# Interleaving the rounded and rest weights of a projection word by word in one SBUF tile

## The chip, the cores and the metric

The kernel runs on one core of a Trainium2 chip. The time is that of the device, in microseconds (us), from one launch; the median of several runs is quoted. A profiled execution of the same program gives the trace: start and length of each instruction on each engine. TensorE (PE in the rows) multiplies, and its weight loads have a track of their own (PEld). ScalarE is ACT, VectorE is DVE, GpSimd is POOL, and SyncE is SP, which here issues DMA transfers.

## The reference

One step of a decoder layer for 256 prompt tokens and 8 sample tokens (264 together) with a model width of 2048. An RMS-normed input goes through a wide input projection. Two branches follow, sparse attention (compressed, selected and window keys, with a cache of 2048 past tokens for each sample) and a gated delta rule. Each branch is gated and projected back, the two are merged by sigmoid gates, and an output projection is added to the residual:

```python
(q_a, kvc, kvs, kvw, g_nsa, z_a, qkv_b, a_b, b_b, z_b, gate_a, gate_b) = split_proj(rms_norm(x_p, norm_w) @ w_in)
...
y_a = nsa_merge(o_cmp, o_slc, o_win, g_nsa, z_a, w_pa)
y_b, S_p, conv_p = gdn_branch(qkv_b, a_b, b_b, z_b, zero_conv, zero_S, *gw)
m = jax.nn.sigmoid(gate_a) * y_a + jax.nn.sigmoid(gate_b) * y_b
return x + m @ w_o
```

The compressed keys and values come from a learned map over the cache: rows of 16 tokens times `w1` (first product), a SiLU, and `w2` (second product).

## The kernel before

All arithmetic is done in float32 quality. A matmul on type `fp32r` keeps fewer bits, so each operand is cut in two: a rounded part (`hi`, a copy on ScalarE to type fp32r) and the rest (`lo`, the original minus `hi`, on VectorE). A product is then three matmuls that add up in PSUM, hi by hi, hi by lo and lo by hi (`three`).

The projections are a list of *half units*, `halves`. A half unit `W` is a block of 1024 rows by 128 columns of a weight matrix (72 columns for the small projection `wsm`), stored as 128 partitions by 8 chunks by 128. Its `load` issues one DMA of 512 KB to the tile `raw`. Its `split` allocates `hi` and `lo` and fills them: one ScalarE copy of 1024 elements per partition (L324) and one VectorE subtraction (L325). Its `mms` runs 24 matmuls, 8 chunks by three products: the weights are `hi[:, k, :]` or `lo[:, k, :]`, the streamed operand is a 264-column slice of `xh`/`xl` (input projection), `oh`/`ol` (branch outputs) or `mh`/`ml` (merged output). In the rows "acc<-xl,hi" is a matmul that streams `xl` past the weights `hi`; weights stand last. All matmuls are issued by the helper at L197, transposes by L194.

`CQ` units do the first product of the compression. There `hi` and `lo` hold the cache rows, 256 or 288 columns for each of 2 to 4 steps, and are streamed; the weights are `w1h` and `w1l`, which were split once. `W` and `CQ` take their `hi` and `lo` from the same tags, with three buffers each. The second product is in `g_cmp_fin`: for values, the weights are `hg[:, g, :]`, where

```python
hg = hs[:, :n].rearrange("p (c g) -> p g c", g=2)
...
mm(p2[0:nn, 128 * g:128 * g + 128], hg[:, g, :], P("w2v"))
```

so these weights (tile `chs`) are every second word of a row. A product of plain float32 operands is two loads and two matmuls in the trace.

The main loop at the end of `program` goes through `halves`: at step i it issues the load of half i + 4, the split of half i + 2, and the matmuls of half i in two parts, and after each part the generators of all other work (attention, delta rule, norms) may advance by one step (`tick`). SP's and GpSimd's queues are written out in program order; the order of instructions on TensorE, ScalarE and VectorE is laid out when the kernel is built.

Of the kernel before, what the change touches and what calls it, by code (L numbers as in the profile page):

```python
# [11 lines left out]
F32R = mybir.dt.float32r  # L12
# [124 lines left out]
def program(tc, A):  # L137
# [4 lines left out]
    def pool(name, bufs=1, space=None):  # L142
        p = tc.tile_pool(name=name, bufs=bufs, space=space) if space is not None else tc.tile_pool(name=name, bufs=bufs)
        ctxs.append(p)
        return p.__enter__()
# [3 lines left out]
    st = pool("st")  # L149
# [163 lines left out]
    class W:  # L313
# [5 lines left out]
            SP.dma_start(self.raw, self.src)  # L319

        def split(self):
            self.hi = st.tile([128, 8, self.cols], F32R, name="hi", tag="hi", bufs=3)
            self.lo = st.tile([128, 8, self.cols], F32R, name="lo", tag="lo", bufs=3)
            S.activation(self.hi, self.raw, AF.Copy)  # L324
            V.tensor_sub(self.lo, self.raw, self.hi)  # L325

# [56 lines left out]
    class CQ:  # L383
# [8 lines left out]
        def split(self):  # L392
            kv, b, s0, s1 = self.kv, self.b, self.s0, self.s1
            n = 256 + 32 * self.prompt
            self.hi = st.tile([128, s1 - s0, n], F32R, name="hi", tag="hi", bufs=3)
            self.lo = st.tile([128, s1 - s0, n], F32R, name="lo", tag="lo", bufs=3)
            for ph in range(2):
                src = rawc[kv, b][ph][:, :, s0:s1].rearrange("p n s c g -> p s n (c g)")
                h = self.hi[:, :, 128 * ph:128 * ph + 128].rearrange("p s (n c) -> p s n c", n=8)
                l = self.lo[:, :, 128 * ph:128 * ph + 128].rearrange("p s (n c) -> p s n c", n=8)  # L400
                S.activation(h, src, AF.Copy)  # L401
                V.tensor_sub(l, src, h)  # L402
            if self.prompt:
                h = self.hi[:, :, 256:].rearrange("p s (c g) -> p s g c", g=2)
                l = self.lo[:, :, 256:].rearrange("p s (c g) -> p s g c", g=2)
                for g in range(2):
                    src = L["kvc"][:, 2 * kv + g, 0:TP].rearrange("p (c s) -> p s c", s=16)[:, s0:s1]
                    S.activation(h[:, :, g], src, AF.Copy)
                    V.tensor_sub(l[:, :, g], src, h[:, :, g])
# [1055 lines left out]
    hl = {}  # L1465
# [145 lines left out]
    n = len(halves)  # L1611
# [117 lines left out]
```

## Time and profile before

| | |
|---|---|
| median of 3 runs | 1151.09 us (1150.13 to 1151.12) |
| profiled execution | 1147.96 us, span of its instructions 1146.2 us |
| matmuls | 9088, TensorE busy 1116.5 us (97%) |
| weight loads | 9088, busy 1090.7 us (95%) |
| VectorE, ScalarE, GpSimd | 777.0, 603.5 and 146.6 us (68%, 53%, 13%) |
| mean granted clock of TensorE | 0.996 of full speed |

Busy time is the union of an engine's instructions. Matmuls overlap in the pipeline, each is recorded longer than the distance to the next, and their ends are modelled: what a matmul costs in a stream is the distance from start to start. The recorded length of a load is longer than its distance to the next load, too.

### The profile page before, as it was taken

To read this page: it belongs to the slowest core of one execution; us is meant where nothing else is said; L and a number is where in the kernel's file an instruction comes from. 1 tells how busy PE (TensorE), PEld (TensorE's weight loads), DVE (VectorE), ACT (ScalarE), POOL (GpSimd) and SP (SyncE) were. 2 spreads that over 40 slices of the span, in tenths; PEclk is the share of its full clock that TensorE was granted. 3 is DMA by queue.
4 is the path that set the end of the run, shared out by engine and by line. 5 is a ranking of instruction groups with operands and counts; after the bars stand their busy time and mean duration, and the time that the engine had idled before them with its cause. 6 is when DMAs were issued, how large, how long until landed. Compare 5 with 4: busy or idle time off the path is not lost.

```text
span 1146.2 us, 24552 instructions
## 1 busy us (share of the span) xinstructions
PE 1116.5 (97%) x9088; PEld 1090.7 (95%) x9088; DVE 777.0 (68%) x1619; ACT 603.5 (53%) x1165; POOL 146.6 (13%) x218
## 2 busy tenths in 40 slices
PE   4999999999999999999899999999999999999998
PEld 4989999999999998998899999999999999999998
DVE  3587665444667886996888977699746685567543
ACT  4455655445635776785566644444344844454332
POOL 4430344200001311114110300100100000000000
PEclk9999999999999999999999999999999999999999
DMA  8874676335536775467996944655752555555673
GB/s 299 256 233 142 195 216 205 124 111 165 169 121 197 210 203 154 127 190 191 261 356 240 330 152 163 180 181 175 214 179 108 212 186 183 185 179 204 213 238 128
DMA packets 76842, 222.74 MB, mean 194 GB/s; under 512 B 10465, under 2 KB 27370, under 8 KB 75186
## 3 DMA queue, kind: packets, MB, share of 16 engines
q1 hardware_dynamic: 59922, 168.55, 45.5%
q0 software_dynamic: 14784, 45.61, 14.0%
q10 hardware_dynamic: 2016, 7.01, 1.6%
q8 instruction: 71, 1.16, 0.4%
q14 instruction: 49, 0.40, 0.1%
HBM read 203.14 MB, written 17.99 MB: 193 GB/s over the span
## 4 chain that ended last, share of the span: by engine, by line
PE 85%; DVE 4%; DMA 3%; issue 1%; ACT 1%; POOL 0%; ACTq 0%; POOLq 0%; DVEq 0%
PE acc L197 70%; DMA gv<-cslv,idx 2%; DVE lo L325 1%; PE po L197 1%; PE gsc L197 1%; PE gtr L194 1%; DVE lanes L1227 1%; PE ps L197 1%; PE sw L197 1%; DMA raw<-win 1%; PE inv L197 1%; PE cf L197 1%; DVE prod L1226 1%; PE pvo L197 1%; PE uw L197 1%
## 5 line engine op out<-in xcount | busy, mean ns | idle before, releaser
L324 ACT ACTIVATE hi<-raw 128x1024 fp32r<-128x1024 f32 (+1 forms) x250 | 264.1, 1056 | 328.4 <-PE acc L197 265.4
L197 PE MATMUL acc<-xh,hi 128*128 128x264 f32 (+1 forms) x1488 | 428.9, 288 | 0.3 <-ACT gate L1491 0.3
L197 PE MATMUL acc<-xl,hi 128*128 128x264 f32 (+1 forms) x1488 | 426.8, 287 | 0.0
L197 PE MATMUL acc<-xh,lo 128*128 128x264 f32 (+1 forms) x1488 | 425.6, 286 | 0.0
L325 DVE TENSOR_TENSOR lo<-raw,hi 128x1024 fp32r<-128x1024 f32 (+1 forms) x250 | 304.3, 1218 | 171.5 <-ACT hi L324 168.7
L197 PEld LDWEIGHTS acc<-xl,hi 128*128 128x128 f32 (+1 forms) x1488 | 280.6, 189 | 2.0 <-issue 0.6
L197 PEld LDWEIGHTS acc<-xh,hi 128*128 128x128 f32 (+1 forms) x1488 | 280.5, 189 | 2.0 <-ACT gate L1491 0.6
L197 PEld LDWEIGHTS acc<-xh,lo 128*128 128x128 f32 (+1 forms) x1488 | 279.6, 188 | 1.7 <-issue 0.5
L197 PE MATMUL acc<-hi,w1h 128*128 128x254 f32 (+1 forms) x512 | 147.7, 289 | 15.9 <-ACT hi L401 15.9
L197 PE MATMUL acc<-lo,w1h 128*128 128x254 f32 (+1 forms) x512 | 146.5, 286 | 3.3 <-DVE lo L402 3.1
L197 PE MATMUL acc<-hi,w1l 128*128 128x254 f32 (+1 forms) x512 | 145.1, 283 | 0.0
L402 DVE TENSOR_TENSOR lo<-rawc,hi 128x512 fp32r<-128x512 f32 (+2 forms) x136 | 84.1, 656 | 52.1 <-ACT hi L401 45.9
L197 PEld LDWEIGHTS acc<-hi,w1h 128*128 128x128 f32 x512 | 97.9, 191 | 16.0 <-ACT hi L401 15.9
L401 ACT ACTIVATE hi<-rawc 128x512 fp32r<-128x512 f32 (+2 forms) x136 | 74.7, 599 | 61.3 <-PE acc L197 56.5
L197 PEld LDWEIGHTS acc<-lo,w1h 128*128 128x128 f32 x512 | 98.6, 192 | 4.5 <-DVE lo L402 4.3
L197 PEld LDWEIGHTS acc<-hi,w1l 128*128 128x128 f32 x512 | 98.3, 192 | 0.1
L378 POOL DMA_DIRECT2D rawc<-ccmp x125 | 67.4, 539 | 97.7 <-issue 72.6
L197 PE MATMUL acc<-oh,hi 128*128 128x264 f32 x256 | 73.6, 287 | 0.2 <-ACT gate L1491 0.2
L197 PE MATMUL acc<-ol,hi 128*128 128x264 f32 x256 | 73.5, 287 | 0.0
L197 PE MATMUL acc<-oh,lo 128*128 128x264 f32 x256 | 73.4, 287 | 0.0
L197 PE MATMUL acc<-mh,hi 128*128 128x264 f32 x256 | 72.7, 284 | 0.0
L197 PE MATMUL acc<-ml,hi 128*128 128x264 f32 x256 | 72.6, 283 | 0.0
(453 smaller groups left out, 1651.9 us busy)
## 6 DMA issues: line engine op xcount, KB each, us to landing
raw<-win SPq DMA_DIRECT2D x184, 512.0 KB, 3.7
raw<-wpab SPq DMA_DIRECT2D x32, 512.0 KB, 3.3
raw<-wo SPq DMA_DIRECT2D x32, 512.0 KB, 3.5
rawc<-ccmp SPq DMA_DIRECT2D x126, 128.0 KB, 3.1
rawc<-ccmp POOLq DMA_DIRECT2D x125, 128.0 KB, 3.3
raw<-w SPq DMA_DIRECT2D x8, 512.0 KB, 5.4
wk<-winK SPq DMA_DIRECT2D x8, 512.0 KB, 9.3
o_wk<-wk POOLq DMA_DIRECT2D x8, 512.0 KB, 8.0
```

What stands on the lines that cost most here:

```text
L194: T.transpose(out, in_, ident[0:n, 0:n])
L197: T.matmul(out, lhsT, rhs, start=start, stop=stop, **k)
L324: S.activation(self.hi, self.raw, AF.Copy)
L325: V.tensor_sub(self.lo, self.raw, self.hi)
L378: e.dma_start(rawc[kv, b][j // 8][:, j % 8].rearrange("p s c g -> p (s c g)"), src[kv, bass.ds(r, 1)].rearrange("o d f -> (o d) f"))
L401: S.activation(h, src, AF.Copy)
L402: V.tensor_sub(l, src, h)
L1226: V.tensor_tensor(pp, Lt[:, 0:i, 0:i], La[:, i, 0:i, None].to_broadcast([64, i, i]), ALU.mult)
L1227: V.tensor_reduce(Lt[:, i, 0:i], pp.rearrange("p j c -> p c j"), AX.X, ALU.add, negate=True)
```

## The change

One tile per half unit takes the place of two. For `W` it is 128 partitions by 8 chunks by 128 columns by 2 words, and `hi` and `lo` are the words 0 and 1 of each pair: 8 bytes lie between one element of `hi` and the next. The copy writes with this stride, the subtraction reads `hi` and writes `lo` with it, and the weight loads read with it. The small projection uses 72 of the 128 columns. For `CQ` the tile holds first all of `hi` and then all of `lo`, each contiguous as before. The tile's tag has three buffers, as each of the two tags had. The bytes in SBUF are the same for 128-column halves.

```diff
         def split(self):
-            self.hi = st.tile([128, 8, self.cols], F32R, name="hi", tag="hi", bufs=3)
-            self.lo = st.tile([128, 8, self.cols], F32R, name="lo", tag="lo", bufs=3)
+            hl = st.tile([128, 8, 128, 2], F32R, name="hilo", tag="hilo", bufs=3)
+            self.hi, self.lo = hl[:, :, 0:self.cols, 0], hl[:, :, 0:self.cols, 1]
             S.activation(self.hi, self.raw, AF.Copy)
             V.tensor_sub(self.lo, self.raw, self.hi)
...
             n = 256 + 32 * self.prompt
-            self.hi = st.tile([128, s1 - s0, n], F32R, name="hi", tag="hi", bufs=3)
-            self.lo = st.tile([128, s1 - s0, n], F32R, name="lo", tag="lo", bufs=3)
+            hl = st.tile([128, 2, s1 - s0, n], F32R, name="hilo", tag="hilo", bufs=3)
+            self.hi, self.lo = hl[:, 0], hl[:, 1]
```

## Rows read from the trace of the kernel before

**Rows 1.** Page, busy time, share of the span, instructions of each engine.

```profile
PE 1116.5 (97%) x9088; PEld 1090.7 (95%) x9088; DVE 777.0 (68%) x1619; ACT 603.5 (53%) x1165; POOL 146.6 (13%) x218
```

**Rows 2.** Page, groups of instructions: count | busy us, mean ns | idle before, releaser.

```profile
L324 ACT ACTIVATE hi<-raw 128x1024 fp32r<-128x1024 f32 (+1 forms) x250 | 264.1, 1056 | 328.4 <-PE acc L197 265.4
...
L325 DVE TENSOR_TENSOR lo<-raw,hi 128x1024 fp32r<-128x1024 f32 (+1 forms) x250 | 304.3, 1218 | 171.5 <-ACT hi L324 168.7
```

**Rows 3.** Chain that ended last, pieces in time: start us, length us, what.

```profile
189.97 11.22 PE acc L197 x96
...
637.14 9.61 DMA raw<-win
...
932.50 210.53 PE acc L197 x1742
```

**Rows 4.** Timeline, 163.5 to 164.6 us: start us, length us, engine, instruction.

```profile
163.55 0.19 PEld L197 LDWEIGHTS acc<-hi,w1l 128*128 128x128 f32 x1
163.66 0.28 PE L197 MATMUL acc<-hi,w1l 128*128 128x254 f32 x1
163.66 0.55 PEld L197 LDWEIGHTS cf<-prm,chs 128*127 128x127 f32 x4
...
163.78 0.63 PE L197 MATMUL cf<-prm,chs 128*127 128x128 f32 x4
```

**Rows 5.** Groups by line, shapes kept apart: weight loads of half units.

```profile
L197 PEld LDWEIGHTS acc<-xl,hi 128*128 128x128 f32 x1472 | 278.3, 189 | 2.0 <-issue 0.6
...
L197 PEld LDWEIGHTS acc<-xl,hi 128*72 128x72 f32 x16 | 2.3, 142 | 0.0
```

**Rows 6.** Timeline of PE, first and last of 31 matmuls, small projection.

```profile
290.76 0.29 PE L197 MATMUL acc<-xh,hi 128*72 128x264 f32 x1
...
294.43 0.29 PE L197 MATMUL acc<-xh,hi 128*72 128x264 f32 x1
```

**Rows 7.** Timeline near 157 us: four loads in a row, few streamed columns.

```profile
157.17 0.53 PEld L197 LDWEIGHTS cf<-csq,cst 128*128 128x128 f32 x4
```

**Rows 8.** Waits: who waited for whom, us in total, times, longest.

```profile
ACT hi L324 <- PE acc L197: 265.4, 163, 6.7
...
PEld acc L197 <- DVE lo L325: 0.2, 1, 0.2
```

**Rows 9.** Instructions of the tile cf: duration ns min/median/max, start first and last.

```profile
L197 PEld LDWEIGHTS cf<-prm,chs x36: 92/196/199, 163.7 to 248.2; 128*127 128x127 f32 x32, 128*15 128x15 f32 x4
...
L197 PEld LDWEIGHTS cf<-cst,csq x32: 187/191/192, 47.7 to 157.9; 128*127 128x127 f32 x32
```

**Rows 10.** Timeline of PE, first and last of 745 matmuls.

```profile
1039.65 0.28 PE L197 MATMUL acc<-ol,hi 128*128 128x264 f32 x1
...
1129.55 0.28 PE L197 MATMUL acc<-ml,hi 128*128 128x264 f32 x1
```

**Rows 11.** Timeline, a half unit's matmul behind two transposes.

```profile
282.58 0.37 PE L197 MATMUL acc<-xl,hi 128*128 128x264 f32 x1
```

**Rows 12.** Groups by line, shapes kept apart: short copies and a subtraction.

```profile
L408 ACT ACTIVATE hi<-kvc 128x48 fp32r<-128x48 f32 x16 | 3.6, 272 | 0.0
...
L1454 ACT ACTIVATE dso<-dod 128x64 f32<-128x64 f32 x1 | 0.3, 254 | 0.0
...
L409 DVE TENSOR_TENSOR lo<-kvc,hi 128x48 fp32r<-128x48 f32 x16 | 3.0, 228 | 0.0
```

**Rows 13.** Lines L1409 and L1412: duration ns min/median/max, start.

```profile
L1409 DVE TENSOR_TENSOR wq<-wq,deb x1: 216/216/216, 664.3 to 664.3; 128x64 f32<-128x64 f32 x1
...
L1412 DVE TENSOR_TENSOR dkq<-dcv x1: 220/220/220, 664.0 to 664.0; 128x64 f32<-128x64 f32 x1
```

**Rows 14.** Timeline, one split of the last stage and its first `lo` matmul.

```profile
1050.18 1.06 ACT L324 ACTIVATE hi<-raw 128x1024 fp32r<-128x1024 f32 x1 [1.47 <-PE acc L197]
...
1051.27 1.23 DVE L325 TENSOR_TENSOR lo<-raw,hi 128x1024 fp32r<-128x1024 f32 x1
...
1056.09 0.28 PE L197 MATMUL acc<-mh,lo 128*128 128x264 f32 x1
```

## The prediction

> **What bounds the kernel now.** I read the page's busy shares first: the matmuls cover 1116.5 of 1146.2 us [rows 1]. The time is a count of matmuls times their spacing, plus some 30 us in which TensorE has nothing to run. For the count I take the groups by line: 250 copies and 250 subtractions make the weights of 250 half units [rows 2], and a half unit has 24 matmuls (`mms`, 8 chunks by three products), together 6000. The chain that ended last gives their spacing: 1742 of them in 210.53 us, 120.9 ns each, with 264 streamed columns; 96 matmuls of the compression take 11.22 us, 116.9 ns each, with 254 [rows 3]. Per streamed column that is 0.458 and 0.460 ns.
>
> A weight load runs beside each matmul. The timeline shows how they interlock: a load starts with the matmul before it or up to 0.01 us later, and the load's own matmul follows 0.11 to 0.12 us after [rows 4]. For this change all hangs on which of the two sets the 121 ns. The small projection tells: its weights have 72 columns, its loads last 142 ns where those of 128 columns last 189 [rows 5], yet 31 of its matmuls start from 290.76 to 294.43 [rows 6], 30 spacings of 122.3 ns. A load 47 ns shorter buys nothing. The matmul sets the spacing and the load has room.
>
> How much room? Loads set the pace where few columns are streamed. Four loads of 128 contiguous columns beside 15 streamed ones cover 0.53 us, the last of them 0.19: (0.53 - 0.19) / 3 = 113 ns from load to load [rows 7]. Against 121 that leaves 8 ns.
>
> The waits show who else could hold TensorE: a load waited 0.2 us, once, for a `lo` of L325, while ScalarE waited 265.4 us, 163 times, until TensorE gave a buffer back [rows 8]. The splits run ahead of their use.
>
> **The change, part by part.** *Loads.* The 6000 loads of the half units are now read with a stride of 8 bytes. The kernel before has loads of just this form: `hg[:, g, :]`, weights of the compression's second product, is every second word of `chs`. With 127 columns they last 196 ns in the median, against 191 for 127 contiguous columns of `csq` [rows 9], and four of them cover 0.55 us [rows 4]: (0.55 - 0.196) / 3 = 118 ns from load to load, against 113. So the stride costs 5 to 6 ns a load; with one column more I take a floor of 118.5 ns. That is 2.5 ns under the mean spacing. The first load of such a group runs beside a 254-column matmul, and the next matmul starts 0.12 us on (163.66 to 163.78 [rows 4]); over the six such places the starts lie 117, 118, 119, 119, 120 and, once, 209 ns apart. That is what a floor near 118.5 gives, beside a matmul at full pace.
>
> The spacings scatter, and those under the floor are lifted to it. The 745 matmuls from 1039.65 to 1129.55, first and last in [rows 10], have a mean spacing of 120.8 ns; 41 spacings are 117 ns or less, 115 are 118 or less. Raising each one under 118.5 to 118.5 adds 0.2 ns to the mean; a floor of 120 would add 0.5 and one of 121 would add 1.0. I take 0.2 ns x 6000 = 1.2 us, with 0 (the stride costs nothing) and 1.0 x 6000 = 6.0 us (the room is used up) as bounds.
>
> Where a half unit resumes behind another kind of matmul, no long matmul hides the load: the one at 282.58, behind two transposes, is recorded 0.37 us long instead of 0.28, since it waits for its weights [rows 11]. The trace has 189 such resumptions; 55 of them follow a matmul of 256 columns or more, which hides the load. The other 134 pay 6 ns each: 0.8 us, from 0 to 1.1 (all 189).
>
> The Trainium skill (SBUF — State Buffer, section "Door 1: The DMA port swizzle") gives SBUF lines of 16 bytes and says that two accesses to a line suffice to absorb its latency. An 8-byte stride leaves just two words per line, so by that page the strided loads are free and the time stays at 1151.1. The 196 against 191 ns of [rows 9] disagree, and the row decides.
>
> *ScalarE.* The copy to `hi` (1056 ns, [rows 2]) now writes with the stride. No row has that alone. The nearest is L408: 48 elements, written 8 bytes apart and read 64 bytes apart, 272 ns; 64 contiguous elements take 254 [rows 12]. Less 16 x 1.03 (1056 / 1024) that is 237 for 48, so L408 pays 35 ns, 0.73 per element. The bounds are 0 and 0.73 x 1024 = 0.74 us a copy.
>
> *VectorE.* The subtraction (1218 ns, [rows 2]) reads `hi` and writes `lo` with the stride. L1409 reads and writes 64 elements 8 bytes apart in 216 ns, and L1412 takes 220 on contiguous ones [rows 13]: nothing. L409 is 48 elements, with another operand read 64 bytes apart: 228 ns [rows 12], against 220 - 16 x 1.19 = 201, so 27 / 48 x 1024 = 0.58 us a subtraction as the upper bound. L1409 has the new form and L409 has a wider stride besides, so I take 0, and by likeness 0 for ScalarE.
>
> Both lie beside matmuls in any case. In the last stage the copy starts at 1050.18, the subtraction lasts from 1051.27 to 1052.50, and that half's first `lo` is used at 1056.09 [rows 14]: 3.6 us of cover, which is also the median when I pair all 250 halves so. At both upper bounds, 1.3 us, all but 9 stay covered. If the cover were gone, TensorE would wait for the copy and the subtraction in turn, 2.3 us.
>
> *The shared tile.* `hi` and `lo` are now given back together, at the latest when the last product has read `lo`, one spacing (0.12 us) after the last use of `hi`. The next split starts that much later, against 3.6 us of cover: 0. If a first product now had to wait for `lo` as well as for `hi`, the same cover holds: 0. In the compression units each part stays contiguous within its tile, and their weights (`w1h`, `w1l`) are not touched: 0. No DMA, no byte and no queue changes.
>
> Sum: 1.2 + 0.8 + 0 = 2.0 us on the profiled execution (1147.96 us, span 1146.2). The median of the runs lies 3.1 above that; I carry the difference over: 1151.1 + 2.0 = **1153.1 us**, 0.17% more. About 0.2%, 2.3 us, is what a measurement of this kernel can tell from no change, so the forecast is no change.
>
> **The rivals.**
> *Slower: the load becomes the pace.* A load begins with its predecessor's matmul or up to 10 ns later [rows 4]; if such a delay comes on top of the 118, the floor is 121 or more, and from there each nanosecond counts 6000 times. A floor of 121.5 adds about 1.3 ns in the mean, 7.8 + 0.8 us: 1160. If the whole 6 ns go onto each spacing it is 36 + 0.8: 1188. For it: there are 2.5 ns of room, measured on few loads. Against it: the 72-column weights and the six 254-column spacings. It decides from 121 ns on. The Trainium skill (TensorE: Matmul & The Clock Gate, section "Back-to-back issue gap") says that in a stream matmul and weight load together set the spacing; by that rule this rival is the case. The 122.3 ns of [rows 6] disagree while the load is the shorter of the two.
>
> *Slower: ScalarE and VectorE.* At the upper bounds, 0.74 + 0.58 us more per half, the nine halves with less cover than that are late by 6.6 us together: 1151.1 + 2.0 + 6.6 = 1160. L1409 speaks against it, L408 for it.
>
> *Faster: another order.* Only the queues of SP and GpSimd are written out by hand; the order on the other engines is laid out at build from the tiles and when they are given back. If one tile per half moves instructions there, a wait in the chain, such as the 9.61 us for `raw` at 637 [rows 3], may shorten; losing 5 us of it gives 1151.1 + 2.0 - 5 = 1148. It could as well grow, and nothing in the trace says that the order moves.
>
> **How the numbers follow.** Hidden loads, as summed: 0.65, with a range of its own from 1150 to 1158; 0.50 of it within 0.2%, 0.15 above. The load as the pace: 0.16. ScalarE and VectorE: 0.09. Another order: 0.10. So faster 0.10, same 0.50, slower 0.15 + 0.16 + 0.09 = 0.40. The range from 1149 to 1163 takes in the bounds of the sum and the near ends of the slower rivals; outside it I leave 0.07 of the faster case and 0.11 of the far ends of the others.
>
> **What would show it.** Right: loads of half units of about 194 instead of 189 ns, spacings of 121.0 to 121.3 ns in the long last piece of the chain, L324 and L325 still at 1056 and 1218. Wrong: a spacing of 122 ns or more there (the load sets the pace); L324 or L325 longer by 0.3 us or more, with new waits of TensorE for them; or stages in another order.

## The result

The kernel got slower: 1162.56 us in the median of four runs (1162.28 to 1164.07), against 1151.11 for the kernel before in four runs beside them. The ratio is 1.0103, with a 95% interval from 1.0086 to 1.0121: 11.45 us, 1.0%. The forecast was 1153.1 us and no change; the range from 1149 to 1163 holds the time.

The profiled execution took 1162.28 us, with a span of 1160.6. First the page's busy shares of the changed kernel, which answer to [rows 1], and its groups of instructions for the two halves of the split, which answer to [rows 2] (count | busy us, mean ns | idle before, releaser):

```profile
PE 1129.5 (97%) x9088; PEld 1103.0 (95%) x9088; DVE 779.8 (67%) x1619; ACT 625.6 (54%) x1165; POOL 146.9 (13%) x218
...
L325 DVE TENSOR_TENSOR hilo<-raw,hilo 128x1024 fp32r<-128x1024 f32 (+1 forms) x250 | 305.2, 1221 | 177.8 <-ACT hilo L324 176.1
L324 ACT ACTIVATE hilo<-raw 128x1024 fp32r<-128x1024 f32 (+1 forms) x250 | 287.3, 1149 | 215.6 <-PE acc L197 171.4
```

TensorE's busy time grew by 13.0 us with the same 9088 matmuls. Its idle time, span less busy, went from 29.7 to 31.1 us. So the loss sits inside the matmul stream, and not in new waits. The waits of TensorE confirm it (total us, times, longest):

```profile
PE acc L197 <- ACT hilo L401: 15.1, 2, 14.1
PE acc L197 <- DVE hilo L402: 4.2, 2, 3.1
PE acc L197 <- DVE gate L1498: 3.8, 3, 2.6
```

None is for L324 or L325; the 14.1 us is the wait for the first cache rows, which the kernel before has too (15.9 us). ScalarE's copy is 93 ns longer than before (1149 against 1056), VectorE's subtraction 3 ns.

Where the matmul stream lost, the chain that ended last shows (start us, length us), as in [rows 3]:

```profile
191.70 11.22 PE acc L197 x96
...
936.60 220.82 PE acc L197 x1798
```

The 96 matmuls of the compression, whose weights are contiguous in both kernels, take 11.22 us as before. The half units in the long last piece take 220.82 / 1798 = 122.8 ns each instead of 120.9. In the windows view, 90 us of that piece have no other work, and TensorE is covered throughout at full clock (columns: window, length, PE, PEld, DVE, ACT, POOL busy, PEclk, DMA share, GB/s):

```profile
1040.00:1130.00 90.00, 90.00 (x736) 90.00 (x735) 52.77 (x69) 38.07 (x40) 0.00 (x0) 1.00 0.63 217
```

The window counts 736 matmuls with those that run over its edges; 733 of them start in it, 122.8 ns apart. Before, 745 started in 89.9 us, 120.8 ns apart [rows 10]. The weight loads of the changed kernel, with shapes kept apart, answer to [rows 5]:

```profile
L197 PEld LDWEIGHTS acc<-xl,hilo 128*128 128x128 f32 x1472 | 287.5, 195 | 1.0 <-issue 0.2
L197 PEld LDWEIGHTS acc<-xl,hilo 128*72 128x72 f32 x16 | 2.3, 144 | 0.0
```

195 instead of 189 ns for 128 columns, and 144 instead of 142 for 72.

From here on a *mean spacing* is worked out from all start times of the trace: the mean from one matmul of a half unit to the next of its kind, with 128 columns of weights, leaving out the pauses (spacings over 1.3 times the median). It is 121.02 ns before and 122.86 after. 1.84 x 6000 = 11.0 us, against 11.45 measured.

### The profile page after: what moved, and what is told of

It is laid out like the page before. It is cut to its first block, busy times and chain, and to the rows that moved or that the text cites. A ratio compares the mean times of both kernels' runs of the same rounds, so it can differ in the third digit from the quotient of the medians.

```text
span 1160.6 us, 24512 instructions
## 1 busy us (share of the span) xinstructions
PE 1129.5 (97%) x9088; PEld 1103.0 (95%) x9088; DVE 779.8 (67%) x1619; ACT 625.6 (54%) x1165; POOL 146.9 (13%) x218
## 4 chain that ended last, share of the span: by engine, by line
PE 83%; DVE 5%; DMA 3%; issue 1%; ACT 1%; POOL 0%; DVEq 0%; ACTq 0%; POOLq 0%
PE acc L197 68%; DMA gv<-cslv,idx 2%; DVE hilo L325 1%; PE po L197 1%; PE gsc L197 1%; PE sw L197 1%; PE gtr L194 1%; DVE lanes L1227 1%; PE ps L197 1%; DMA raw<-win 1%; PE inv L197 1%; PE pvo L197 1%; PE cf L197 1%; PE uw L197 1%; PE wsc L197 1%
## 5 line engine op out<-in xcount | busy, mean ns | idle before, releaser
L197 PE MATMUL acc<-xh,hilo 128*128 128x264 f32 x2976 | 582.7, 290 | 0.9 <-ACT gate L1491 0.9
L197 PEld LDWEIGHTS acc<-xh,hilo 128*128 128x128 f32 x2976 | 483.0, 195 | 4.1 <-ACT gate L1491 1.2
L197 PE MATMUL acc<-xl,hilo 128*128 128x264 f32 (+1 forms) x1488 | 429.2, 289 | 0.0
L325 DVE TENSOR_TENSOR hilo<-raw,hilo 128x1024 fp32r<-128x1024 f32 (+1 forms) x250 | 305.2, 1221 | 177.8 <-ACT hilo L324 176.1
L324 ACT ACTIVATE hilo<-raw 128x1024 fp32r<-128x1024 f32 (+1 forms) x250 | 287.3, 1149 | 215.6 <-PE acc L197 171.4
L197 PEld LDWEIGHTS acc<-xl,hilo 128*128 128x128 f32 (+1 forms) x1488 | 289.8, 195 | 1.0 <-issue 0.2
L197 PE MATMUL acc<-hilo,w1h 128*128 128x254 f32 (+1 forms) x1024 | 191.8, 288 | 19.7 <-ACT hilo L401 15.1
L197 PEld LDWEIGHTS acc<-hilo,w1h 128*128 128x128 f32 x1024 | 161.5, 192 | 21.5 <-ACT hilo L401 15.3
L197 PE MATMUL acc<-hilo,w1l 128*128 128x254 f32 (+1 forms) x512 | 145.2, 284 | 0.0
L197 PEld LDWEIGHTS acc<-hilo,w1l 128*128 128x128 f32 x512 | 98.4, 192 | 0.1
```

The costliest lines, as they stand in the source:

```text
L197: T.matmul(out, lhsT, rhs, start=start, stop=stop, **k)
```

## The experiments

The expectations call the theories by letters. **A**: a strided load needs about 118 ns from load to load, and the matmul's 121 ns are too near to that; the loss is a matter of the margin between the two. **B**: each strided load costs the stream a fixed 1.8 ns, whatever stands beside it. **C**: the strided writes of ScalarE and VectorE disturb the stream. **D**: the shared tile, with its joint release and another order of instructions, costs the time. D was open, since the order did change: the matmuls of the two kernels first differ at the 694th of 9088. All ratios are against the kernel before on the same chip in the same hour (1148.40 us for the first four experiments, 1148.31 for the next four, 1148.79 for the last four).

### One shared tile, everything contiguous

```diff
-            self.hi = st.tile([128, 8, self.cols], F32R, name="hi", tag="hi", bufs=3)
-            self.lo = st.tile([128, 8, self.cols], F32R, name="lo", tag="lo", bufs=3)
+            hl = st.tile([128, 2, 8, self.cols], F32R, name="hilo", tag="hilo", bufs=3)
+            self.hi, self.lo = hl[:, 0], hl[:, 1]
```

`CQ` is edited as in the change, and the matmuls run in the order of the changed kernel.

> One tile for hi and lo, but all of hi first and then all of lo, so nothing is strided. Theories: (A) the strided load has become the pace of the half units' matmuls, (B) a strided load slows the matmul that streams beside it, (C) the strided writes of ScalarE (1152 instead of 1059 ns) and the waits behind them cost the time, (D) the shared tile, its joint release and the new order of instructions do. A, B and C: 1151 us, within 2 us of the kernel before, spacing in the last stage 121 ns. D: 1160 to 1163 us.

Measured: 1150.77 us, ratio 1.0019 (0.9996 to 1.0041). The last piece of its chain and its loads:

```profile
925.96 136.12 PE acc L197 x1126
```

```profile
L197 PEld LDWEIGHTS acc<-xl,hilo 128*128 128x128 f32 x1472 | 278.3, 189 | 1.2 <-issue 0.2
```

136.12 / 1126 = 120.9 ns; the mean spacing is 121.03. Sharing the tile, releasing both parts together and the order that follows leave the spacing alone. In the time they cost nothing that can be measured; the interval leaves room for 0.4% at most. D falls as the cause of the loss.

### Stride of 8 bytes, two tiles

Each tile interleaves two chunks of its own, so tags, releases and order stay those of the kernel before.

```diff
+            hi = st.tile([128, 4, self.cols, 2], F32R, name="hi", tag="hi", bufs=3)
+            self.hi = [hi[:, k // 2, :, k % 2] for k in range(8)]
+            hi = hi.rearrange("p a c b -> p a b c")
...
+            raw = self.raw.rearrange("p (a b) c -> p a b c", b=2)
+            S.activation(hi, raw, AF.Copy)
+            V.tensor_sub(lo, raw, hi)
```

`lo` likewise.

> Two tiles as before, but in each the columns of two neighbouring chunks are interleaved word by word, so all copies, subtractions and loads of half units have the stride of 8 bytes and nothing is shared. A, B and C: about 1162 us, spacing about 122.9 ns in the half units. D: 1151 us.

Measured: 1159.43 us, ratio 1.0079 (1.0055 to 1.0103).

```profile
943.28 213.90 PE acc L197 x1742
```

```profile
L197 PEld LDWEIGHTS acc<-xl,hi 128*128 128x128 f32 x1472 | 288.4, 196 | 1.9 <-issue 0.6
```

122.8 ns a matmul in the chain, mean spacing 122.83, with the order of matmuls of the kernel before. The stride alone brings the whole rise of the spacing.

### The writes strided, the loads contiguous

The tiles and the split as in the experiment above; the loads take 128 neighbouring words of the same tile (so they read the wrong columns).

```diff
+            f = hi.rearrange("p a c b -> p (a c b)")
+            self.hi = [f[:, self.cols * k:self.cols * k + self.cols] for k in range(8)]
```

> The same two interleaved tiles, written with the stride of 8 bytes, but the loads take 128 contiguous words, so each load holds 64 columns of each of two chunks: the products are of wrong columns, the work is the same. A and B: 1151 us with loads of 189 ns and a spacing of 121 ns, though ScalarE's copy is still 1150 ns long. C: 1160 us or more.

Measured: 1148.27 us, ratio 0.9997 (0.9976 to 1.0019).

```profile
932.55 129.31 PE acc L197 x1070
```

```profile
L331 ACT ACTIVATE hi<-raw 128x1024 fp32r<-128x1024 f32 x248 | 285.3, 1150 | 311.6 <-PE acc L197 234.1 <-issue 45.4 <-DMA raw<-win 8.3
...
L197 PEld LDWEIGHTS acc<-xl,hi 128*128 128x128 f32 x1472 | 278.1, 189 | 2.0 <-issue 0.7
```

The copy (L331 here) is as long as in the changed kernel, 1150 ns, and the spacing is 120.9 ns in that piece and 121.00 in the mean over the trace. (Contiguous loads gave 121.02 before and 121.03 in the first experiment, strided ones 122.86 and 122.83, so the number repeats to 0.03 ns.) The strided writes cost TensorE nothing that can be measured, neither by their length nor by traffic in SBUF. C falls; what is left is the strided load.

### Stride of 16 bytes

As the second experiment, with four chunks interleaved: `[128, 2, self.cols, 4]`, `k // 4`, `k % 4`.

> Four chunks interleaved in each of the two tiles: stride 16 bytes for copies, subtractions and loads, result unchanged. If a load pays for each word that is alone in its 16 bytes (A with the line rule of the Trainium skill, SBUF page), loads are clearly longer than 195 ns, the spacing follows them to 150 ns or more, and the time is above 1300 us. If the price of a strided load is the same for any stride, 1162 us. C would show as a longer copy at an unchanged spacing.

Measured: 1807.02 us, ratio 1.5724 (1.5662 to 1.5785).

```profile
1393.69 407.96 PE acc L197 x1742
```

```profile
L329 ACT ACTIVATE hi<-raw 128x1024 fp32r<-128x1024 f32 x248 | 510.8, 2060 | 686.7 <-PE acc L197 555.5 <-issue 130.0 <-ACT xh L302 0.7
L330 DVE TENSOR_TENSOR lo<-raw,hi 128x1024 fp32r<-128x1024 f32 x248 | 505.6, 2039 | 519.0 <-ACT hi L329 500.8 <-PE qtr L194 18.0
...
L197 PEld LDWEIGHTS acc<-xl,hi 128*128 128x128 f32 x1472 | 485.7, 330 | 1.2 <-issue 0.4
...
L197 PEld LDWEIGHTS acc<-xl,hi 128*72 128x72 f32 x16 | 3.6, 222 | 0.0
```

The load now plainly sets the pace: 407.96 / 1742 = 234.2 ns a matmul, and the loads start 233 ns apart. Behind the 72-column weights the same matmul takes 134.5 ns. So the cost of the stride lies in reading the words of the load, and from 8 to 16 bytes it leaps: the 128-column load goes 189, 195, 330 ns, the copy on ScalarE 1056, 1149, 2060, the subtraction on VectorE 1218, 1221, 2039. Those two, some 4.1 us per half together, still lie under a half unit of 24 x 0.234 = 5.6 us.

The Trainium skill (SBUF — State Buffer, section "Door 1: The DMA port swizzle") gives lines of 16 bytes, and two accesses to a line as enough. The leap between two words in 16 bytes and one word in 16 bytes agrees with it in place; that the 8-byte stride is free holds for VectorE alone here (1221 against 1218 ns).

### 240 streamed columns, contiguous and with the stride

To lay the load's pace bare, the matmuls of the chunks 1 to 7 stream 240 of the 264 columns; chunk 0 keeps 264. (The last 24 tokens get a part of their sum only.) The second kernel adds the two strided tiles.

```diff
+                n = TT if k == 0 else 240
+                three(u["ps"][0:self.cols], self.hi[:, k, :], self.lo[:, k, :], h[:, self.kc0 + k, 0:n],
+                      l[:, self.kc0 + k, 0:n], self.first and k == 0, self.last and k == 7, n)
```

> Half units stream 240 instead of 264 columns in seven of eight chunks (5250 of 6000 matmuls; the last 24 tokens get a part of the sum only), weights contiguous as before. By columns the matmul would take 0.458 x 240 = 110 ns, so the contiguous load's 113 ns should be the pace: some 7 ns less on 5250 matmuls, about 1112 us. The partner of the next kernel.

> The same with the weights of both tiles strided by 8 bytes. A (the strided load is the pace): the shorter matmul gains almost nothing, spacing 118 to 122 ns, 1140 to 1160 us, 30 to 48 us more than its contiguous partner; the spacing is the load's floor. B (a strided load slows the matmul beside it by a fixed share): spacing 1.9 ns above the partner's, 11 us more than the partner.

Measured: contiguous 1119.92 us, ratio 0.9771 (0.9735 to 0.9807); strided 1142.65 us, ratio 0.9956 (0.9937 to 0.9974). The long last pieces of the two chains, the contiguous kernel first:

```profile
908.96 203.10 PE acc L197 x1791
```

```profile
921.41 212.94 PE acc L197 x1791
```

Mean spacings of the 240-column matmuls: 112.16 ns contiguous, 118.17 strided. So the floor of a strided 128-column load is 118.2 ns, where the prediction had 118.5, and a stream that is faster than that takes its pace. With 72-column weights the strided stream of 240 columns runs at 111.4 ns: it is the number of words that the load reads. The contiguous stream runs at 110.8 ns behind the 72-column weights, so contiguous loads of 128 columns, too, hold 240 streamed columns back by 1.3 ns.

The spacing came as A had it, the times did not: 1119.92 us against the 1112 expected, and a pair 22.7 us apart where A gave 30 to 48. A fixed 1.8 ns (B) gives 11; the spacings give 6.0 x 5250 + 2.7 x 750 = 33.5. In the profiled executions the distances from one half-unit matmul to the next, pauses included, add up to 719.5 us before, 680.5 contiguous and 708.4 strided, and all that is left of the span to 426.7, 434.7 and 429.1. So the pair is 27.9 us apart in the half units, and the faster kernel loses 5.6 of that in the rest of the program. Why is not shown: TensorE waits 6.2 us for splits in both. B falls by the spacing, 6.0 ns and not 1.8.

### 288 and 272 streamed columns, contiguous and with the stride

The other side: three of four chunks stream 24, or 8, columns more, which lie behind their own and go to columns of PSUM that nobody reads.

```diff
+                n, c = TT if k % 4 == 3 else 288, TT * (self.kc0 + k)
+                hf, lf = (t.rearrange("p k t -> p (k t)") for t in (h, l))
+                three(u["ps"][0:self.cols], self.hi[:, k, :], self.lo[:, k, :], hf[:, c:c + n],
```

> Half units stream 288 columns in six of eight chunks (4500 of 6000 matmuls; the 24 further columns go to columns of PSUM that nobody reads, so the result stays), weights contiguous. 0.458 x 288 = 132 ns, 11 ns more on 4500 matmuls: about 1200 us. The partner of the next kernel.

> The same with the weights of both tiles strided by 8 bytes. A: a floor of 118 to 123 ns lies under 132, so 4500 loads are hidden again and only the 1500 matmuls of 264 columns still pay 1.9 ns: about 3 us more than the contiguous partner. B: 11 us more, as with 264 columns.

> Half units stream 272 columns in six of eight chunks (4500 matmuls), weights contiguous: 0.458 x 272 = 124.6 ns, 3.6 ns more on 4500 matmuls, about 1165 us. The partner of the next kernel.

> The same with both tiles strided by 8 bytes. With 6.4 ns between the load's floor of 118.2 and the matmul: if the rise comes from loads and matmuls that scatter about nearly equal lengths (pace), it is between the 1.85 ns at 264 columns and the 0.6 at 288, 0.8 to 1.2 ns, 4 to 7 us more than the partner in all. If a strided load slows its matmul by a fixed amount (contention), 1.85 ns and 11 us.

Measured: with 288 columns 1198.54 us contiguous (ratio 1.0448, 1.0416 to 1.0480) and 1201.55 strided (1.0461, 1.0442 to 1.0481), 3.0 us apart. With 272 columns 1167.16 (1.0171, 1.0148 to 1.0193) and 1170.90 (1.0199, 1.0177 to 1.0222), 3.7 us apart, a little under the 4 to 7 that were expected. The long last pieces, 272 contiguous and then 272 strided:

```profile
936.88 225.66 PE acc L197 x1805
```

```profile
944.38 226.71 PE acc L197 x1805
```

With the four pairs together, the rise of the mean spacing by the stride stands against the margin, the contiguous spacing less the strided load's 118.2 ns:

| streamed columns | contiguous, ns | strided, ns | rise, ns | margin, ns |
|---|---|---|---|---|
| 240 | 112.16 | 118.17 | 6.0 | -6.0 |
| 264 | 121.02 | 122.86 | 1.84 | 2.8 |
| 272 | 125.79 | 126.69 | 0.90 | 7.6 |
| 288 | 132.78 | 133.38 | 0.60 | 14.6 |

The rise falls with the margin, as A says; it does not end where the margin passes the scatter of the spacings (a standard deviation of 2.7 ns before), but fades.

The 3.0 us of the 288-column pair are the number that A gave, but they come from elsewhere. A had the 288-column matmuls pay nothing and the 1500 of 264 columns beside them 1.9 ns each. In the traces the first pay 0.60 ns (4500 x 0.60 = 2.7 us) and the second 0.10 (122.27 to 122.37). The same 264-column matmuls pay 0.55 ns among those of 272 columns and 2.69 among those of 240. So what a matmul pays depends on the margin of its neighbours as well as on its own.

### Only one of the two parts strided

In each product group the weights follow as `hi`, `hi`, `lo`. The two kernels interleave only `lo`, or only `hi`, by two chunks.

```diff
+            hi = st.tile([128, 8, self.cols], F32R, name="hi", tag="hi", bufs=3)
+            self.hi = [hi[:, k, :] for k in range(8)]
...
+            lo = st.tile([128, 4, self.cols, 2], F32R, name="lo", tag="lo", bufs=3)
+            self.lo = [lo[:, k // 2, :, k % 2] for k in range(8)]
```

> Only lo strided by 8 bytes (one load of three), hi contiguous. The earlier runs left a mean rise of 1.85 ns at 264 columns, where a floor of 118.2 under a spacing of 121.0 explains some 0.6. If all strided loads pay alike: 11 / 3 = 3.7 us more than before. If the rise belongs to the matmul beside the load, as the changed kernel shows it (3.4 ns while the load of lo runs, 0.8 and 1.2 beside the two loads of hi): 2000 x 3.4 = 6.8 us, and the spacings beside the loads of hi stay at 121.6 and 120.9 ns.

> Only hi strided by 8 bytes (two loads of three), lo contiguous. All alike: 7.4 us more than before. By the matmul beside the load: 2000 x (0.8 + 1.2) = 4 us, and the spacing beside the load of lo stays at 120.6 ns.

Measured: `lo` alone 1158.20 us, ratio 1.0084 (1.0059 to 1.0108); `hi` alone 1155.98 us, ratio 1.0063 (1.0035 to 1.0091). The loads in the last stage, `lo` alone and then `hi` alone:

```profile
L197 PEld LDWEIGHTS acc<-mh,lo 128*128 128x128 f32 x256 | 50.4, 197 | 0.0
...
L197 PEld LDWEIGHTS acc<-mh,hi 128*128 128x128 f32 x256 | 48.2, 188 | 0.0
```

```profile
L197 PEld LDWEIGHTS acc<-mh,hi 128*128 128x128 f32 x256 | 50.2, 196 | 0.0
...
L197 PEld LDWEIGHTS acc<-mh,lo 128*128 128x128 f32 x256 | 48.3, 189 | 0.0
```

Only the strided loads are longer, so the length belongs to the load that reads with the stride. The loss doesn't divide so: one strided load in three raises the mean spacing by 1.72 ns, two in three by 1.23, all three by 1.84. By the place in the group (from the start of the named product to the next start), in ns:

| | `h` x `hi` | `l` x `hi` | `h` x `lo` |
|---|---|---|---|
| before | 121.63 | 120.52 | 120.92 |
| `lo` strided | 122.29 | 122.52 | 123.42 |
| `hi` strided | 123.50 | 122.24 | 121.04 |
| changed kernel | 122.47 | 124.01 | 122.06 |

Strided `hi` slows the two products with `hi` and leaves the third alone; strided `lo` slows all three. Neither a charge per strided load nor one by the matmul that such a load stands beside gives these numbers. What couples neighbouring products this way stays open.

None of these kernels beats the kernel before at the full work.

## Where the forecast held and where it failed

The stated range held the time, by 0.4 us at its upper end, and only because it took in the near ends of the slower rivals. The sum's own range, 1150 to 1158, missed it, and 1.0% is beyond the 0.2% that the prediction took for no change. As far as the sum goes, the hit was luck.

**What the prediction had right.** TensorE's stream is the bound, and the time is a count times a spacing. The strided load is 6 to 7 ns longer (195 and 196 against 189), where 5 to 6 were forecast, and its floor of 118.5 ns, taken from loads of `chs` [rows 4, 9], is 118.2 in the 240-column experiment. VectorE's term of 0 is right (1221 against 1218 ns). The shared tile at 0 is right within the interval of the first experiment, and the order, which did change, costs nothing that can be measured. ScalarE's copy was taken at no change and is 93 ns longer, within the bounds of 0 and 0.74 us; the cover hides it, as the third experiment shows. The 72-column argument [rows 6] holds on: after the change these matmuls run at 121.3 ns, not slower than the 122.4 before, since their loads keep their room.

**What failed: the lift.** The prediction raised each spacing under 118.5 ns to 118.5 and got 0.2 ns x 6000 = 1.2 us. Measured are 1.84 ns x 6000 = 11.0 us, beyond the upper bound of 6.0 that it gave. The rule behind it was the mean over the larger of two numbers, spacing or floor. That the load's pace scatters as well explains some of it only: drawing a spacing from the kernel before and a load-to-load distance from the strided 240-column kernel, each by itself, and taking the larger gives 0.56 ns. That leaves 1.3 ns, which draws that are independent of each other don't give. A load starts with its predecessor's matmul or up to 10 ns later, and the next matmul starts behind its load. That delays of the one are passed on to the other when they are so near in length is argued from these rows, from the fading rise (1.84, 0.90, 0.60 ns) and from the 264-column matmuls that pay by their neighbours; no run shows the step itself. Nor is it excluded that a strided load slows the matmul beside it a little by its reading alone; at 288 columns that is 0.6 ns at most.

**The rival that came.** "The load becomes the pace" gave 1160 us, from a floor of 121.5 ns. The time is near that and so is its sign, with spacings of 122 ns and more in the last piece, as its mark said; but the floor is 118.2 and not 121.5, and the pace is set by both. The Trainium skill (TensorE: Matmul & The Clock Gate, section "Back-to-back issue gap") has matmul and weight load together set the spacing in a stream; the 122.8 ns beside a 118.2 ns load agree with it, where the 72-column rows, with the load well below, could not tell.

**What misled.** The six 254-column matmuls beside a strided load were read as a matmul at full pace. (The one of 209 ns runs beside a load of 15 columns.) Each of them is followed by a short stream, so each shows a single first load that had a contiguous one before it. A delay that is handed on through a long stream can't show there. Two more such places stand behind matmuls of 286 and 264 columns: 137 ns after a spacing of 131, and 123 after 121. There the matmul is longer than the floor, and the spacing rose all the same; two places prove little beside a scatter of 2.7 ns, but they pointed the other way. The 113 ns of [rows 7] are a mean, too, of 118, 108 and 112 ns, and the first of the three runs beside a 254-column matmul. Without it one contiguous load follows the other after about 110 ns, and the stride adds 7 to 8 ns to that rather than 5 to 6. That doesn't enter the sum.

**The other terms.** The count of resumptions is a little off: 64 of the 189, not 55, follow a matmul of 256 columns or more, which makes 0.75 us of the 0.8. With two strided tiles in the order of before, the distance to the resuming matmul is unchanged in the mean (-0.1 ns), and the next one is 4.3 ns longer, which is a part of the 1.84 ns. The other slower rival (ScalarE and VectorE at their upper bounds) did not come: 0.10 instead of 1.3 us more per half, and no wait of TensorE for them. The faster one (another order) did not either. The 1.84 ns give 11.0 of the 11.45 us in the medians. The two profiled executions lie 14.3 apart; 3.1 of that is how far the one before lay under its own median.

## What to carry to other kernels

Don't take a hidden operation for free because it is the shorter one: 3 ns short of a 121 ns matmul, the strided load still cost 1.8 ns each time, and 15 ns short of a 133 ns matmul still 0.6. Keep the words of a weight slice contiguous; if two parts must share a tile, put them side by side, which cost nothing measurable, and interleave, if at all, beside longer streams (0.6 ns at 288 columns) and not with one word in 16 bytes (1.57 times the time here).

## What the runs showed of the hardware

- A load of 128 fp32r columns takes 189, 195 and 330 ns with its words 4, 8 and 16 bytes apart. Where the load sets the pace, one follows the other after 118 ns at 8 bytes and 233 at 16; contiguous ones of plain float32 after 108 and 112 beside 15 streamed columns.
- ScalarE's copy to a strided output of 1024 elements takes 1056, 1149 and 2060 ns, VectorE's subtraction, which reads one operand and writes with the stride, 1218, 1221 and 2039 ns.
- The spacing where matmul and load are nearly equal lies above both: 122.8 ns from 121.0 and 118.2.
